# Splitting the q, k and v weights: from VectorE and POOL to ScalarE and VectorE

## The chip, the cores and the metric

The kernel runs on one core of a Trainium2 chip. The metric is the device time of one execution in microseconds (us). The core has a matrix engine (TensorE, PE in the profile), three engines for element-wise work (VectorE = DVE, ScalarE = ACT, GpSimd = POOL) and SyncE (SP), which issues most of the transfers. Each engine works through its own queue of instructions in order; semaphores hold an instruction back until what it needs is there.

## What is computed

Two layers of a transformer over 256 context and 256 latent tokens, width 1024. Each layer has a mixer with three branches (gated delta rule, RG-LRU, differential attention) and a SwiGLU. All branches begin with one projection of the normalised input, `u @ w_in`. What this case is about is the part of it that the delta-rule branch consumes first:

```python
SPLIT = (DN_W, DN_W, DN_H * DN_DV, ...)          # q, k, v: 512 columns each
pc = split_cols(u_c @ w_in)
pl = split_cols(u_l @ w_in)
...
qkv = jax.nn.silu(centred_dwconv(jnp.concatenate([q, k, v], axis=-1), conv_w))
q, k, v = jnp.split(qkv, [DN_W, 2 * DN_W], axis=-1)
q = l2norm(q.reshape(B, T, DN_H, DN_DK))
k = l2norm(k.reshape(B, T, DN_H, DN_DK))
...
g = -jnp.exp(a_log) * jax.nn.softplus(a + dt_bias)   # later: cumsum within chunks
```

## The kernel before

Activations lie with their 1024 features on partitions (8 tiles of 128) and the 512 tokens along the row (context first). Weights come as slabs of 128 output columns: one slab is 128 x 1024 fp32, 0.5 MB, read by SP into a tile `wr` (line 261, three buffers). To keep fp32 accuracy with faster matmuls, both operands are split into a high part in a rounded format and a low part, the rest: `hi` is `wr` rounded (tile `wh`, three buffers, line 264), `lo = wr - hi` (tile `wl`, two buffers, line 265). The product is three matmuls for each of the 8 row blocks: high by high (line 276), high by the activation's low part (line 277), low by high (line 278), so 24 matmuls of 512 columns a slab (256 for q in layer 1, where only latent tokens go on). The activation's parts are `uh` and `ul` (lines 384 to 392).

Which engine rounds and which subtracts is set by the dictionary `how`, whose lists are cycled slab by slab. `how` is updated at the beginning of each stage; the program's order is rearranged by a scheduler at build time, in which the split of a slab has a raised priority (an offset of 400 at line 262) and its load 300.

The stage concerned is `proj` as called by `qkv` and for W_AB and the first LX slab: k, q, v, then the first slab of the RG-LRU. In layer 0 the slabs of W_AB and k are done within the start-up (lines 456 to 465, tiles `whi`, `wlo`, four quarters), in layer 1 those of W_AB and the first k slab at the end of the layer before (`by_halves`); these don't use this entry of `how`. So 9 slabs in layer 0 and 12 in layer 1 go by it.

After each slab's matmuls `conv` empties PSUM twice on ScalarE (`xp`, line 567, and `ta`, line 569; POOL only sets the borders, lines 565 and 566), adds three taps on VectorE (line 573), ScalarE takes a tanh (line 597, `tb`) and VectorE multiplies (line 598, into `kn`, `qn` or `sv`). Psum banks alternate between `mm` and `pg`. Beside this run the units of the modulation weights (`mod_unit`: 1 MB loads `wm` at line 299, matmuls at line 309, a copy `mev` on ScalarE at line 315, transposes at line 318, small VectorE work on `modT` at lines 320 to 328), the softplus of the decay (lines 538 to 546 and 623 to 631), its two cumulative scans (lines 636 and 637, tile `tc`), whose result PE transposes at line 648, and the norms of k and q: squares at line 510, their sums on PE at line 514, scaling at line 604. `sv` is transposed to tokens at line 682.

Of the kernel before, what the change touches and what calls it, by code (L numbers as in the profile page):

```python
# [178 lines left out]
def build(tc, I, out, dbg=None):  # L179
    nc = tc.nc  # L180
    V, S, G, PE, SP = nc.vector, nc.scalar, nc.gpsimd, nc.tensor, nc.sync
# [71 lines left out]
    how = {"hi": [S], "lo": [V]}  # L253
# [220 lines left out]
    for l in range(L):  # L474
# [98 lines left out]
                V.scalar_tensor_tensor(yv, in0=xp[:, :, j:j + 256], scalar=w[:, j:j + 1], in1=yv, op0=ALU.mult, op1=ALU.add)  # L573


        how.update(hi=[V], lo=[G])
        rot[:] = ["mm", "pg"]
        ab = proj(W_AB, ALL)
        spa = tt("tc", WT)
# [657 lines left out]
```

## Time and profile before

| | |
|---|---|
| time, median of 3 runs | 1825.97 us (1821.45 to 1826.0) |
| the profiled execution | 1825.1 us, span 1823.2 us |
| mean granted TensorE clock | 0.983 |
| PE busy, share of the span | 1704.4 us, 93% |
| VectorE busy | 1086.1 us, 60% |
| ScalarE busy | 812.3 us, 45% |
| POOL busy | 263.6 us, 14% |
| `wl` on POOL (line 265) | 32 times, 84.1 us |
| `wh` on VectorE (line 264) | 84 times, 63.1 us |

The busy times are of the whole program, with stages of very different limits; the stage of the change lies at 25 to 165 us and at 1112 to 1225 us. An instruction counts as busy from its start to its end, whatever it does in between.

### The profile page before, as it was taken

Reading aid. Unit: us, or ns where it says so; the run is one execution under the profiler, and the core shown is the slowest. Engines: PE = TensorE matmul, PEld = TensorE weight load, DVE = VectorE, ACT = ScalarE, POOL = GpSimd, SP = SyncE. Lnnn points to the kernel's source line nnn. Section 1 sums busy time; section 2 is a strip of 40 time slices with the busy share of each in tenths; the row PEclk is TensorE's granted clock in tenths of the full one; section 3 lists DMA queues with packets and bytes.
Section 4 is the critical chain, followed back from the end, with each engine's and each line's share of the span. In section 5 each row is a group of like instructions: output and inputs, shape, how many; then the busy total and the mean of one; then the engine's idle time right before and its main releaser. Section 6 shows DMA issues by size and latency. Waiting matters only on the chain.

```text
span 1823.2 us, 27735 instructions
## 1 busy us (share of the span) xinstructions
PE 1704.4 (93%) x10978; PEld 1394.7 (76%) x10978; DVE 1086.1 (60%) x1746; ACT 812.3 (45%) x1416; POOL 263.6 (14%) x291
## 2 busy tenths in 40 slices
PE   6888999999999999999999998788999999999997
PEld 3556787655788887788888886567878679979997
DVE  4677888585453345533333348778885786765554
ACT  4445755553442233332222233347664644444442
POOL 2322000000120013211110004322201002211100
PEclk9999999999999999999999999889999999999999
DMA  9673111435232343323223345432113226555553
GB/s 334 197 250 120 56 47 36 153 116 185 89 97 93 102 146 125 124 93 104 93 94 100 104 136 168 154 105 72 47 46 107 83 88 223 186 180 181 184 185 128
DMA packets 116066, 233.79 MB, mean 128 GB/s; under 512 B 7216, under 2 KB 73148, under 8 KB 115296
## 3 DMA queue, kind: packets, MB, share of 16 engines
q1 hardware_dynamic: 106736, 227.14, 38.4%
q10 hardware_dynamic: 9200, 4.88, 1.0%
q8 instruction: 86, 1.41, 0.3%
q14 instruction: 44, 0.36, 0.1%
HBM read 229.42 MB, written 2.58 MB: 127 GB/s over the span
## 4 chain that ended last, share of the span: by engine, by line
PE 67%; issue 12%; DVE 11%; ACT 5%; DMA 3%; POOL 2%; SPq 0%; POOLq 0%; DVEq 0%; ACTq 0%
PE mm L277 10%; PE mm L276 10%; PE mm L278 10%; PE dn L278 6%; PE dn L276 6%; PE dn L277 6%; PE dn L777 5%; DMA wm<-in_wmod 2%; PE pp L974 1%; PE pg L278 1%; DVE wl L265 1%; DVE ta L573 1%; PE pg L276 1%; PE pg L277 1%; PE md L309 1%
## 5 line engine op out<-in xcount | busy, mean ns | idle before, releaser
L265 DVE TENSOR_TENSOR wl<-wr,wh 128x1024 fp32r<-128x1024 f32 (+1 forms) x270 | 330.1, 1223 | 414.3 <-PE dn L278 171.5
L264 ACT CAST wh<-wr 128x1024 fp32r<-128x1024 f32 (+1 forms) x218 | 225.4, 1035 | 430.1 <-PE mm L277 133.0
L276 PE MATMUL mm<-uh,wh 128*128 128x512 f32 (+1 forms) x1056 | 378.5, 359 | 8.8 <-ACT wh L264 2.6
L277 PE MATMUL mm<-ul,wh 128*128 128x512 f32 (+1 forms) x1056 | 376.8, 357 | 1.9 <-DVE ul L386 1.4
L278 PE MATMUL mm<-uh,wl 128*128 128x512 f32 (+1 forms) x1056 | 374.3, 354 | 4.4 <-DVE wl L265 3.7
L276 PEld LDWEIGHTS mm<-uh,wh 128*128 128x128 f32 x1056 | 203.1, 192 | 37.4 <-issue 6.4
L277 PEld LDWEIGHTS mm<-ul,wh 128*128 128x128 f32 x1056 | 203.0, 192 | 32.7 <-issue 9.4
L278 PEld LDWEIGHTS mm<-uh,wl 128*128 128x128 f32 x1056 | 202.7, 192 | 27.9 <-DVE wl L265 4.3
L277 PE MATMUL dn<-ul,wh 128*128 128x512 f32 (+1 forms) x448 | 151.9, 339 | 0.0
L278 PE MATMUL dn<-uh,wl 128*128 128x512 f32 (+1 forms) x448 | 151.7, 339 | 0.0
L276 PE MATMUL dn<-uh,wh 128*128 128x512 f32 (+1 forms) x448 | 151.6, 338 | 0.0
L265 POOL TENSOR_TENSOR wl<-wr,wh 128x1024 fp32r<-128x1024 f32 x32 | 84.1, 2629 | 139.6 <-PE mm L278 70.2
L277 PEld LDWEIGHTS dn<-ul,wh 128*128 128x128 f32 x448 | 85.2, 190 | 9.5 <-issue 0.4
L276 PEld LDWEIGHTS dn<-uh,wh 128*128 128x128 f32 x448 | 85.1, 190 | 9.4 <-issue 0.4
L278 PEld LDWEIGHTS dn<-uh,wl 128*128 128x128 f32 x448 | 85.3, 190 | 9.2 <-DVE wl L265 0.2
L264 DVE CAST wh<-wr 128x1024 fp32r<-128x1024 f32 x84 | 63.1, 751 | 47.5 <-PE mm L277 30.3
L282 POOL TENSOR_TENSOR hid<-ft,hid 128x512 fp32r<-128x512 f32 (+1 forms) x44 | 44.8, 1018 | 318.8 <-ACT hid L281 318.8
L278 PE MATMUL dn<-hid,wl 128*128 128x256 f32 (+1 forms) x198 | 62.9, 318 | 1.7 <-DVE wl L265 1.7
L276 PE MATMUL mm<-hid,wh 128*128 128x256 f32 (+1 forms) x198 | 62.9, 318 | 0.0
L276 PE MATMUL dn<-hid,wh 128*128 128x256 f32 (+1 forms) x198 | 62.9, 318 | 0.0
L278 PE MATMUL mm<-hid,wl 128*128 128x256 f32 (+1 forms) x198 | 62.9, 318 | 0.0
L278 PE MATMUL pg<-uh,wl 128*128 128x512 f32 (+1 forms) x168 | 62.6, 373 | 0.2 <-POOL wl L265 0.2
(362 smaller groups left out, 3480.2 us busy)
## 6 DMA issues: line engine op xcount, KB each, us to landing
wr<-in_w SPq DMA_DIRECT2D x284, 512.0 KB, 3.8
wm<-in_wmod SPq DMA_DIRECT2D x44, 1024.0 KB, 7.6
wr<-in_w SPq DMA_DIRECT2D x18, 384.0 KB, 3.6
r<-rd SPq DMA_DIRECT2D x5, 1024.0 KB, 5.3
ta<-gd ACTq DMA_DIRECT2D x16, 256.0 KB, 3.6
wm<-in_wmod SPq DMA_DIRECT2D x16, 256.0 KB, 5.3
w<-in_w SPq DMA_DIRECT2D x4, 640.0 KB, 10.3
h<-in_hin SPq DMA_DIRECT2D x8, 256.0 KB, 3.0
```

Of the source, the lines that this page charges most:

```text
L264: (eh.copy if eh is S else eh.tensor_copy)(hi[:, k], r32[:, k])
L265: el.tensor_tensor(lo[:, k], in0=r32[:, k], in1=hi.bitcast(F32)[:, k], op=ALU.subtract)
L276: PE.matmul(ps, lhsT=hi[:, k], rhs=xh[:, tk], start=first and i == 0, stop=False)
L277: PE.matmul(ps, lhsT=hi[:, k], rhs=xl[:, tk], start=False, stop=False)
L278: PE.matmul(ps, lhsT=lo[:, k], rhs=xh[:, tk], start=False, stop=last and i == n - 1)
L282: (eng or G).tensor_tensor(lo, in0=y, in1=hi.bitcast(F32), op=ALU.subtract)
L309: mm = PE.matmul(ps[j:j + 32], lhsT=s_act[:, k], rhs=ts[k // n][:, k % n], start=k < 4, stop=k >= 4, tile_position=(0, j))
L573: V.scalar_tensor_tensor(yv, in0=xp[:, :, j:j + 256], scalar=w[:, j:j + 1], in1=yv, op0=ALU.mult, op1=ALU.add)
L777: PE.matmul(p[:, j], lhsT=lhs[:, j], rhs=rhs[:, j], start=True, stop=True)
L974: PE.matmul(p[:, n], lhsT=gw[:, n, j], rhs=lx[:, j], start=True, stop=True)
```

## The change

One line sets other engines for this stage; the same 21 slabs are split, into the same tiles.

```diff
-        how.update(hi=[V], lo=[G])
+        how.update(hi=[S], lo=[V])
         rot[:] = ["mm", "pg"]
         ab = proj(W_AB, ALL)
```

`V` is VectorE, `G` POOL, `S` ScalarE. The rounding (line 264) becomes a copy on ScalarE, the subtraction (line 265) a VectorE instruction. Since the scheduler orders every queue anew, the split's instructions don't simply change place. Three places show it. The numbers behind a tile's name tell one use of a buffer from another.

VectorE in layer 0's start-up, in the second of the four quarters, where `wh_795` and `wl_796` belong to the first q slab:

```order
-L384 SCALAR_TENSOR_TENSOR nt_279<-h_96,am_82,nrs_171 128x256
-L264 CAST wh_795<-wr_794 128x1024
-L384 SCALAR_TENSOR_TENSOR nt_279<-h_96,am_82,nrs_171 128x256
-L386 SCALAR_TENSOR_TENSOR ul_105<-nt_279,modT_80,uh_104 128x256
-L390 TENSOR_SCALAR nt_286<-nt_286,am_82,modT_80 128x256
-L386 SCALAR_TENSOR_TENSOR ul_105<-nt_279,modT_80,uh_104 128x256
-L390 TENSOR_SCALAR nt_286<-nt_286,am_82,modT_80 128x256
+L384 SCALAR_TENSOR_TENSOR nt_279<-h_96,am_82,nrs_171 128x256 x2
+L390 TENSOR_SCALAR nt_286<-nt_286,am_82,modT_80 128x256 x2
+L265 TENSOR_TENSOR wl_796<-wr_794,wh_795 128x1024
+L386 SCALAR_TENSOR_TENSOR ul_105<-nt_279,modT_80,uh_104 128x256 x2
```

The cast is gone from between the two products `nt`; the subtraction stands behind both `nt` of the odd block and ahead of both `ul`.

VectorE in layer 1 from line 540 on, the run-up to the scans (`wh_10011`, `wl_10012`: the last q slab; 9968 and 9969 the q slab before it; 10056 and 10057 the first v slab):

```order
 L540 TENSOR_SCALAR tb_9825<-ta_9824 128x520
-L264 CAST wh_10011<-wr_10010 128x1024
+L265 TENSOR_TENSOR wl_9969<-wr_9967,wh_9968 128x1024
 L598 SCALAR_TENSOR_TENSOR kn_9565<-tb_9775,ta_9774 128x512
-L320 TENSOR_REDUCE modT_81<-md_9814 128x4
 L321 TENSOR_TENSOR modT_81<-modT_81,vec 128x4
 L325 SCALAR_TENSOR_TENSOR am_85<-modT_81,vec 128x4
+L265 TENSOR_TENSOR wl_10012<-wr_10010,wh_10011 128x1024
 L543 SCALAR_TENSOR_TENSOR tb_9825<-tb_9825,ta_9824 128x520
-L264 CAST wh_10056<-wr_10055 128x1024
 L544 TENSOR_TENSOR tb_9825<-tb_9825,tc_9823 128x520
 L545 SCALAR_TENSOR_TENSOR tb_9826<-tc_9563,tb_9826 128x520
```

Each cast of a slab is replaced by the subtraction of the slab one or two earlier; further down, up to the scans, two more casts (`wh_10117`, `wh_10166`) go and two more subtractions (`wl_10057`, `wl_10118`) come.

ScalarE at the same place in layer 1:

```order
-L315 COPY mev_9812<-md_9803 128x256
+L264 CAST wh_10011<-wr_10010 128x1024
 L541 ACT_TABLE_LOAD
 L541 ACTIVATE tb_9826<-tb_9825 128x520
-L510 ACTIVATE sq_9893<-kn_9565 128x2048
+L264 CAST wh_10056<-wr_10055 128x1024
 L542 ACT_TABLE_LOAD
 L542 ACTIVATE tc_9823<-tb_9826 128x520
+L510 ACTIVATE sq_9893<-kn_9565 128x2048
+L264 CAST wh_10117<-wr_10116 128x1024
 L567 COPY xp_9913<-pg_9852 128x256
```

Three casts come in between the tanh of the last k slab and the first copy of q; the squares of `kn` move behind the second table load, and the copy `mev_9812` has moved ahead of the tanh of line 597. A fourth cast, `wh_10166`, stands ahead of the copy of line 631, which the first scan needs.

## Rows read from the trace of the kernel before

**Rows 1.** Busy time by stretch: length; PE, PEld, DVE, ACT, POOL (instructions); clock; DMA; GB/s

```profile
25.00:60.00 35.00, 31.32 (x182) 20.02 (x182) 18.63 (x48) 11.53 (x32) 15.14 (x14) 0.95 0.73 247
60.00:165.00 105.00, 92.64 (x569) 61.35 (x568) 74.63 (x131) 50.95 (x84) 24.84 (x44) 0.98 0.68 222
1112.00:1165.00 53.00, 45.03 (x304) 33.41 (x305) 37.55 (x54) 17.77 (x33) 23.76 (x26) 0.97 0.58 188
1165.00:1185.00 20.00, 12.58 (x74) 9.24 (x73) 16.81 (x22) 8.97 (x14) 9.17 (x10) 0.80 0.34 107
1185.00:1225.00 40.00, 31.43 (x138) 25.16 (x138) 33.29 (x45) 19.21 (x32) 11.37 (x18) 0.88 0.32 106
```

**Rows 2.** Instructions of lines 265 and 264: count, then ns least/median/most, first and last start

```profile
L265 DVE TENSOR_TENSOR wl<-wr,wh x270: 951/1224/1921, 150.2 to 1807.2; 128x1024 fp32r<-128x1024 f32 x126, 128x768 fp32r<-128x768 f32 x9
...
L265 POOL TENSOR_TENSOR wl<-wr,wh x32: 2371/2666/2911, 32.9 to 1388.3; 128x1024 fp32r<-128x1024 f32 x32
...
L264 ACT CAST wh<-wr x218: 816/1053/1073, 451.4 to 1804.3; 128x1024 fp32r<-128x1024 f32 x100, 128x768 fp32r<-128x768 f32 x9
L264 DVE CAST wh<-wr x84: 666/687/2901, 32.1 to 1514.7; 128x1024 fp32r<-128x1024 f32 x84
```

**Rows 3.** Timeline of POOL in layer 1: start, us, engine, line, operation [idle before <-releaser]

```profile
1165.97 2.40 POOL L265 TENSOR_TENSOR wl<-wr,wh 128x1024 fp32r<-128x1024 f32 x1
```

**Rows 4.** Timeline of VectorE, same columns, around that and elsewhere

```profile
33.10 2.61 DVE L386 SCALAR_TENSOR_TENSOR ul<-nt,modT,uh 128x256 fp32r<-128x256 f32 x1
...
35.96 0.47 DVE L386 SCALAR_TENSOR_TENSOR ul<-nt,modT,uh 128x256 fp32r<-128x256 f32 x1
...
1166.02 2.90 DVE L264 CAST wh<-wr 128x1024 fp32r<-128x1024 f32 x1
...
1176.25 3.35 DVE L636 TENSOR_TENSOR_SCAN tc<-tb,tc 4x512 f32<-4x512 f32 x1
1179.63 1.22 DVE L637 TENSOR_TENSOR_SCAN tc<-tb,tc 4x512 f32<-4x512 f32 x1
...
1218.93 2.83 DVE L573 SCALAR_TENSOR_TENSOR ta<-xp,vec,ta 128x512 f32<-128x512 f32 x1
```

**Rows 5.** PE's waits, 1090 to 1245 us: us in total, times, longest

```profile
PE dn L648 <- DVE tc L637: 7.1, 1, 7.1
PE dn L682 <- DVE sv L598: 4.7, 1, 4.7
PE dn L514 <- ACT sq L510: 3.9, 1, 3.9
PE md L318 <- ACT mev L315: 3.2, 2, 1.7
PE md L309 <- DMA wm<-in_wmod: 2.0, 1, 2.0
```

**Rows 6.** PE's waits, 25 to 185 us

```profile
PE dn L514 <- ACT sq L510: 4.2, 1, 4.2
PE mm L277 <- DVE ul L386: 3.4, 2, 1.7
...
PE md L309 <- ACT ta L569: 1.6, 1, 1.6
```

**Rows 7.** The chain that ended last, in order of time: start us, us, what

```profile
1184.14 0.43 PE pg L276
...
1187.44 0.23 PE pg L278
```

**Rows 8.** VectorE's waits, 25 to 165 us

```profile
DVE wh L264 <- PE mm L277: 4.7, 2, 2.8
...
DVE wh L264 <- PE pg L277: 3.2, 3, 1.7
```

**Rows 9.** VectorE's waits, 1112 to 1240 us

```profile
DVE wh L264 <- PE pg L277: 5.3, 3, 3.0
...
DVE wh L264 <- PE mm L277: 4.1, 3, 2.5
```

## The prediction

> **What bounds the kernel now.** The change touches two stretches, about 25 to 165 us (layer 0) and 1112 to 1225 us (layer 1); so the first view is the busy time of each engine by stretch [rows 1]. PE is busy there for 31.32 of 35, 92.64 of 105, 45.03 of 53, 12.58 of 20 and 31.43 of 40 us: nearly full in layer 0, far from it between 1165 and 1225, where VectorE is busy for 16.81 of 20 and 33.29 of 40 us and the granted clock is down to 0.80 and 0.88. In layer 1's projections VectorE sets the pace.
>
> Much of this VectorE time is no work. POOL's low-part subtraction takes 2.67 us (median of 32), the same operation on VectorE 1.22 us [rows 2]. Now lay POOL's and VectorE's instructions of the same microseconds side by side [rows 3, 4]: POOL subtracts from 1165.97 to 1168.37, and VectorE's cast of line 264, begun at 1166.02, takes 2.90 us instead of 0.69. The scan of line 636 takes 3.35 us, its twin of line 637 behind it 1.22. `ul` takes 2.61 us at 33.10 and 0.47 us at 35.96. While POOL subtracts, a VectorE instruction that begins is held until POOL ends. The list of waits doesn't show this, because the held instruction counts as busy. I went through VectorE's instructions beside all 21 POOL subtractions that the change removes and took from each stretched one the duration of its like that ran alone: 22 instructions, the first at 33.10, the last at 1218.93, hold 41.6 us too much (15.9 in layer 0, 25.7 in layer 1).
>
> Third, what this does to PE: the list of PE's waits. Layer 1 [rows 5]: 7.1 us for the scan (line 637 before the transposes of line 648), 4.7 for `sv`, 3.9 for the squares that hang on `kn`, 3.2 for `mev`, 2.0 for a load of `wm`. Layer 0 [rows 6]: 4.2 for the squares, 3.4 for `ul`, 1.6 for `ta`. Behind long waits matmuls of 512 columns step at 0.43 us instead of 0.23 [rows 7]: that is the lower of the two levels, 1.2 against 2.4 GHz.
>
> **The change, part by part.** 21 slabs are concerned: layer 0 has W_AB and the k slabs from the start-up, so 9 (q, v, the first LX); layer 1 has W_AB and the first k slab from its entry, so 12.
>
> POOL loses 21 x 2.67 = 56 us. VectorE loses 21 casts of 0.69 and gains 21 subtractions of 1.22 [rows 2], +11.1 us, and loses the 41.6 us of being held: 30.5 us less. ScalarE gains 21 casts of 1.05 [rows 2], 22.1 us; it is busy for 50.95 of 105 us and for 8.97 of 20 and 19.21 of 40 us [rows 1], so there is room but no free passage, since its queue is in order.
>
> What of this lies on PE's path, by stretch:
>
> 25 to 60: the order shows `wl` ahead of `ul` on VectorE in two of the three quarters. Before, `ul` came behind a cast and its own holding, 0.69 + 2.14 us; after, behind a 1.22 us subtraction, so 1.6 us earlier, twice: 3.2 of the 3.4 us of waits.
>
> 60 to 165: the wait for `ta` (1.6) hangs on a `kn` product that is held for 2.2 us; taken whole. The wait for the squares (4.2) has three held instructions ahead of it (6.5 us), against which three subtractions cost 3 x 0.53 more: 4.9 earlier at most; I take 3, since ScalarE has two more casts there. Sum 4.6.
>
> 1112 to 1165: the `wm` load (2.0) was issued late because SP's queue is in order and stood on buffers that POOL freed late; `mev` (3.2) stood behind a tanh that waited for held convolutions, and in the new order it is ahead of that tanh. I take 4 of 5.2.
>
> 1165 to 1185: between line 540 and the scans four instructions are held, 8.7 us together. Four subtractions in the place of four casts cost 2.1 more there, and two of the new ScalarE casts (`wh_10056` ahead of the second table load, `wh_10166` ahead of the copy that the scan needs) another 2.1: 8.7 - 2.1 - 2.1 = 4.5 of the 7.1 us.
>
> 1185 to 1225: four held instructions (8.0 us) against 4 x 0.53: 5.9 of the 8.6 us.
>
> Sum of waits 3.2 + 4.6 + 4 + 4.5 + 5.9 = 22.2 us. **The clock**: by the granted means [rows 1] the low level cost at most 0.05 x 35 + 0.02 x 105 + 0.03 x 53 + 0.20 x 20 + 0.12 x 40 = 14.2 us, part of it while PE stood still; it fell behind the waits that shrink. Between 0 and 14.2 I take 5, since waits of 2 to 3 us stay.
>
> **What it gives back**: a new cast waits in ScalarE's queue until PE has let go of the slab three back, and at several places stands just ahead of the copy out of PSUM (lines 567 and 569) of the slab that PE has just finished. The same wait stood in VectorE's queue: 4.7, 3.2, 5.3 and 4.1 us [rows 8, 9]. In its place VectorE's new subtraction waits for PE's end of the slab two back, which is about the same moment; I cost this move at nothing, and if that cover is missing it costs those 17.3 us. The casts themselves: of 19 not yet counted one in five on the path, 19 x 1.05 / 5 = 4 us; the bounds are 0 and 20 us.
>
> The sum: 22.2 + 5 - 4 = 23 us less. The profiled execution took 1825.1 us, 0.9 under the median of the three; 1826.0 - 23 = **1803 us**.
>
> A rule speaks against the change: the Trainium skill (Perfetto Trace Analysis, Optimizing Scalar/DVE Operations) has it that what VectorE does in one of its faster modes should stay there unless VectorE is saturated. The trace agrees on the price (0.69 against 1.05 us) [rows 2]; VectorE at 84% with a third of it held [rows 1] is not saturated by work, so by the rule the cast should have stayed and only the subtraction moved, and the change would lose 21 x 0.37 = 7.8 us that I count only where a cast is on the path.
>
> **Rivals.** (a) PE's clock recovers wholly: 22.2 + 14.2 = 36 us, 1790 us. For it: the low level stands only behind the named waits. Against: 2 to 3 us of wait are left at the scan and the squares. (b) ScalarE takes over as the engine waited for: its casts on the path give back 14 to 27 us of the 27.2, 1813 to 1826 us. For it: it evacuates every slab, and its queue is in order. Against: under 49% busy in these stretches [rows 1]. (c) Slower: the casts and the waits in front of them come onto the path whole, 22.1 + 17.3 = 39.4 us against 22.2 + 5 gained: 12 us more, 1838 us. The place is layer 1 from the k slabs to the scans, where tanh, softplus and evacuation share ScalarE; it decides from the point at which more than 27 of these 39 us are on PE's path. Against it: a wait by PE for VectorE or ScalarE is 7.1 us at the longest now, and the cast is away from VectorE at every such place. (d) The loads set the pace: PE comes earlier to the `wm` units than their 1 MB loads (one wait for DMA of 2.0 us [rows 5], and a DMA share of 0.68 in layer 0 [rows 1]); then layer 0's 4.6 and the 4 of 1112 to 1165 go, and with them the clock: 23 - 13.6 = 9 us, 1817 us. That the change wouldn't do what it says is out: the order has no subtraction of these slabs on POOL any more.
>
> **How the numbers follow.** Forecast (1793 to 1812) 0.60; (a) 0.15; (b) 0.15, a third of it within 0.3%; (c) 0.05; (d) 0.05. 0.3% (5.5 us) is about what a measurement of this kernel can tell from no change. Faster by more: 0.60 + 0.15 + 0.10 + 0.05 = 0.90; within: 0.05; slower: 0.05. The range reaches to (a) and into (b) and (d): 1788 to 1817 us.
>
> **What would show it.** In the profile after: POOL's group of line 265 has 11 instructions left; VectorE has no scan of 3.35 us and no 2.6 us `ul`; its busy time falls by some 30 us and ScalarE's rises by 22; PE's wait for line 637 falls from 7.1 to about 3 us and the granted clock between 1165 and 1225 rises over 0.9. The prediction is wrong if PE's waits name ScalarE's `xp` or `ta` instead, if the held VectorE instructions turn out to have had slack behind them, or if the other POOL instructions hold VectorE as much as the removed ones.

## The result and the profile after

The changed kernel takes 1792.47 us (median of 4 runs, 1790.19 to 1794.81) against 1825.99 us before in the same comparison: ratio 0.983, 95% interval 0.981 to 0.985, 33.5 us less. The forecast was 1803, the range 1788 to 1817. A second comparison gave 1796.4 us for the same kernel, ratio 0.984 (0.982 to 0.986): between two comparisons the changed kernel moves by 4 us, so 30 to 34 us are gained.

First the engines over the whole program, from the page of the changed kernel (busy time, share of the span of 1788.4 us, instructions):

```profile
PE 1692.2 (95%) x10978; PEld 1390.1 (78%) x10978; DVE 1063.0 (59%) x1746; ACT 830.6 (46%) x1437; POOL 207.2 (12%) x270
```

PE runs the same 10978 matmuls in 1692.2 us instead of 1704.4, and stands still for 1788.4 - 1692.2 = 96.2 us instead of 1823.2 - 1704.4 = 118.8. So of the 34.8 us of the profiled executions 12.2 are PE's busy time and 22.6 are waits. The 12.2 us are the clock: the mean granted clock is 0.990 after and 0.983 before, and PE's busy time times the granted clock is about 1675 us in both. VectorE's busy time fell by 23.1 us, ScalarE's rose by 18.3, POOL's fell by 56.4.

Busy time by stretch, the answer to [rows 1] (the same columns; each stretch is cut where PE has run as many matmuls as at the borders there, to within a few, so it lies earlier):

```profile
25.50:54.50 29.00, 28.72 (x183) 19.27 (x182) 19.36 (x49) 13.79 (x37) 11.09 (x12) 1.00 0.85 290
54.50:151.50 97.00, 90.79 (x568) 61.21 (x568) 67.92 (x131) 55.98 (x90) 5.91 (x38) 1.00 0.73 241
1095.30:1140.50 45.20, 43.40 (x306) 33.69 (x306) 30.15 (x55) 23.11 (x38) 7.95 (x21) 0.96 0.69 222
1140.50:1153.90 13.40, 10.87 (x74) 8.76 (x72) 11.40 (x17) 9.83 (x15) 0.34 (x4) 1.00 0.48 157
1153.90:1191.20 37.30, 29.44 (x142) 23.43 (x139) 29.43 (x47) 23.21 (x38) 4.07 (x17) 0.92 0.34 113
```

PE stands still for 0.3, 6.2, 1.8, 2.5 and 7.9 us of these stretches; before it was 3.7, 12.4, 8.0, 7.4 and 8.6. The granted clock is 1.00 in three of the five. Only the last stretch waits about as long as before, at a clock of 0.92 against 0.88.

Lines 265 and 264, the answer to [rows 2]:

```profile
L265 DVE TENSOR_TENSOR wl<-wr,wh x291: 951/1225/3394, 33.3 to 1772.8; 128x1024 fp32r<-128x1024 f32 x137, 128x768 fp32r<-128x768 f32 x9
...
L265 POOL TENSOR_TENSOR wl<-wr,wh x11: 2367/2432/2759, 679.1 to 1354.4; 128x1024 fp32r<-128x1024 f32 x11
```

```profile
L264 ACT CAST wh<-wr x239: 817/1053/1067, 31.4 to 1770.0; 128x1024 fp32r<-128x1024 f32 x111, 128x768 fp32r<-128x768 f32 x9
L264 DVE CAST wh<-wr x63: 662/686/696, 132.6 to 1480.5; 128x1024 fp32r<-128x1024 f32 x63
```

21 subtractions left POOL, which keeps 11, and 21 casts went to ScalarE. Before, the longest VectorE cast took 2901 ns; now the longest takes 696.

VectorE's timeline at the places of [rows 4] (start us, us, engine, line, operation):

```profile
34.43 1.85 DVE L386 SCALAR_TENSOR_TENSOR ul<-nt,modT,uh 128x256 fp32r<-128x256 f32 x2
...
1150.10 1.20 DVE L636 TENSOR_TENSOR_SCAN tc<-tb,tc 4x512 f32<-4x512 f32 x1
1151.34 1.22 DVE L637 TENSOR_TENSOR_SCAN tc<-tb,tc 4x512 f32<-4x512 f32 x1
```

The first scan takes 1.20 us instead of 3.35. Two `ul` together take 1.85 us; alone they take 0.87, so here 1.0 us of holding is left, beside POOL's own `ul` of line 392, which the change leaves alone.

PE's waits in layer 1, 1070 to 1225 us, the answer to [rows 5] (total, times, longest):

```profile
PE dn L682 <- DVE sv L598: 6.5, 2, 4.6
...
PE dn L514 <- ACT sq L510: 1.4, 1, 1.4
PE dn L648 <- DVE tc L637: 1.4, 1, 1.4
PE pg L276 <- ACT ta L569: 1.2, 1, 1.2
```

and in layer 0, 25 to 180 us, the answer to [rows 6]:

```profile
PE dn L682 <- DVE sv L598: 2.3, 1, 2.3
...
PE md L318 <- ACT mev L315: 1.7, 2, 1.0
PE mm L276 <- ACT uh L385: 1.3, 1, 1.3
PE mm L277 <- DVE ul L386: 1.1, 1, 1.1
```

The wait for the scan has fallen from 7.1 to 1.4 us, those for the squares from 4.2 and 3.9 to 0 and 1.4, the one for the `wm` load from 2.0 to 0.3; the one for `sv` in layer 1 has grown, from 4.7 to 6.5. In both stretches together all of PE's waits add up to 40.9 us before and 19.7 after.

### The profile page after: what moved, and what is told of

The parts are those of the page before. It is cut to its first block, busy times and chain, and to the rows that moved or that the text cites. A ratio compares the mean times of both kernels' runs of the same rounds, so it can differ in the third digit from the quotient of the medians.

```text
span 1788.4 us, 27733 instructions
## 1 busy us (share of the span) xinstructions
PE 1692.2 (95%) x10978; PEld 1390.1 (78%) x10978; DVE 1063.0 (59%) x1746; ACT 830.6 (46%) x1437; POOL 207.2 (12%) x270
## 4 chain that ended last, share of the span: by engine, by line
PE 69%; issue 11%; DVE 10%; ACT 5%; DMA 3%; POOL 1%; SPq 0%; POOLq 0%; ACTq 0%; DVEq 0%
PE mm L277 10%; PE mm L276 10%; PE mm L278 10%; PE dn L278 7%; PE dn L276 7%; PE dn L277 7%; PE dn L777 5%; DMA wm<-in_wmod 2%; DVE wl L265 1%; PE pg L277 1%; PE pg L278 1%; PE pg L276 1%; PE pp L974 1%; PE md L309 1%; PE dn L309 1%
## 5 line engine op out<-in xcount | busy, mean ns | idle before, releaser
L265 DVE TENSOR_TENSOR wl<-wr,wh 128x1024 fp32r<-128x1024 f32 (+1 forms) x291 | 358.7, 1233 | 430.6 <-PE dn L278 176.2
L264 ACT CAST wh<-wr 128x1024 fp32r<-128x1024 f32 (+1 forms) x239 | 247.5, 1036 | 438.2 <-PE mm L277 139.9
L276 PE MATMUL pg<-uh,wh 128*128 128x512 f32 (+1 forms) x168 | 62.0, 369 | 1.2 <-ACT ta L569 1.2
L276 PE MATMUL mm<-hid,wh 128*128 128x256 f32 (+1 forms) x198 | 62.9, 318 | 0.0
L276 PE MATMUL dn<-hid,wh 128*128 128x256 f32 (+1 forms) x198 | 62.9, 318 | 0.0
L277 PE MATMUL mm<-hid,wh 128*128 128x256 f32 (+1 forms) x198 | 62.6, 316 | 0.0
L277 PE MATMUL dn<-hid,wh 128*128 128x256 f32 (+1 forms) x198 | 62.5, 316 | 0.0
```

Source lines behind the costliest of these rows:

```text
L264: (eh.copy if eh is S else eh.tensor_copy)(hi[:, k], r32[:, k])
L265: el.tensor_tensor(lo[:, k], in0=r32[:, k], in1=hi.bitcast(F32)[:, k], op=ALU.subtract)
L276: PE.matmul(ps, lhsT=hi[:, k], rhs=xh[:, tk], start=first and i == 0, stop=False)
L277: PE.matmul(ps, lhsT=hi[:, k], rhs=xl[:, tk], start=False, stop=False)
```

## The experiments

The theory, H: a POOL instruction that reads tiles makes a VectorE instruction that begins meanwhile stand until it ends, and most of the gain is the end of that. Two rivals: L, the low part and the buffers `wr` and `wl` were late because POOL was slow, and PE and the loads waited for that; W, VectorE simply had too much to do.

All times stand beside runs of the kernel before on the same chip, which took 1826.0 to 1826.9 us. "PE idle" is the span minus PE's busy time. The busy and idle times are those of the one profiled execution, which can lie some us off the median: after's is the fastest of its four (1790.2 us) and e9's of its four (1794.8), e8's is the slowest of its four (1845.8).

| kernel | us, median | ratio, 95% | PE busy | PE idle | VectorE busy |
|---|---|---|---|---|---|
| before | 1826.0 | 1 | 1704.4 | 118.8 | 1086.1 |
| after | 1792.5 | 0.981 to 0.985 | 1692.2 | 96.2 | 1063.0 |
| e12, after again | 1796.4 | 0.982 to 0.986 | 1695.8 | 100.1 | 1063.2 |
| e1, cast alone | 1818.9 | 0.994 to 0.998 | 1707.9 | 112.2 | 1069.8 |
| e2, subtraction alone | 1799.1 | 0.984 to 0.987 | 1697.8 | 103.5 | 1066.5 |
| e5, idle subtraction | 1807.8 | 0.987 to 0.991 | 1698.0 | 108.3 | 1089.3 |
| e6, idle memsets | 1796.7 | 0.982 to 0.985 | 1695.6 | 100.3 | 1063.1 |
| e8, two idle subtractions | 1841.1 | 1.006 to 1.009 | 1718.5 | 125.5 | 1121.1 |
| e9, start-up back | 1799.9 | 0.983 to 0.988 | 1694.6 | 98.4 | 1061.2 |
| e4, layer 1 alone | 1807.7 | 0.988 to 0.992 | 1701.3 | 108.2 | 1067.6 |
| e7, POOL splits no slab here | 1790.6 | 0.979 to 0.982 | 1694.7 | 94.1 | 1060.3 |
| e10, `ul` too | 1792.1 | 0.980 to 0.984 | 1694.5 | 95.7 | 1058.3 |
| e11, all low parts | 1789.0 | 0.978 to 0.982 | 1696.0 | 92.0 | 1097.7 |

**Each half alone.** The rounding alone (e1), the subtraction alone (e2):

```diff
-        how.update(hi=[V], lo=[G])
+        how.update(hi=[S], lo=[G])   # e1
+        how.update(hi=[V], lo=[V])   # e2
```

> Half of the change: the cast goes to ScalarE, the subtraction stays on POOL. VectorE loses 21 x 0.69 = 14 us of work, nothing else. Theory H: the held time stays, so little comes of it, 1815 to 1826 us. Rival W (VectorE's load is what counts, whatever takes it off): 14 of 30 us of relief, so about half of the gain, 1806 to 1812 us.

> The other half: the cast stays on VectorE, the subtraction goes from POOL to VectorE. VectorE gets 21 x 1.22 = 26 us of work more and loses the 42 us of being held. Theory H: 16 us of VectorE's time net, about half to most of the gain, 1796 to 1808 us. Rival W (what helps is work that leaves VectorE for an engine with room): VectorE has more to do than before, 1826 us or above.

e1 gained 7 us, e2 27. In e2 VectorE has all of the work, 21 casts and 21 subtractions, so W, by which it had too much to do, falls: taking work off VectorE (e1) is worth a quarter of giving it more without POOL (e2). PE's waits in layer 1 of e1, 1090 to 1245 us:

```profile
PE pg L276 <- ACT ta L569: 5.2, 1, 5.2
PE dn L682 <- DVE sv L598: 5.2, 2, 4.0
PE dn L514 <- ACT sq L510: 3.9, 1, 3.9
```

The squares are as late as in [rows 5], 3.9 us: POOL still subtracts. What the cast adds to e2 is 3 to 7 us by the medians. Up to the end of layer 0's projections and from line 581 to 728 in layer 1 the traces of e2 and after differ by only 1.1 us (148.05 against 148.85 us, and 88.2 against 86.3); the other 11.8 us of the two spans arise outside these stretches, where the two profiles of the changed kernel also differ by 7.5 us, and the intervals of e2 and after overlap. So the cast's share is small and not settled. By the Trainium skill (Perfetto Trace Analysis, Optimizing Scalar/DVE Operations) a VectorE performance mode is faster where there is one, and moving work to ScalarE may make sense if VectorE is saturated; with VectorE busy for 59% that speaks for e2. The run shows nothing of the 7.8 us by which e2 would then be faster: it is 3 to 7 us slower by the medians.

**An idle reader on POOL.** e5 is the changed kernel with one useless subtraction on POOL for each slab of this stage. It waits only for the slab's cast, touches a tile of its own, nobody waits for it, and the queues of PE, VectorE, ScalarE and SP hold the same instructions in the same order as after. e6 has three memsets in its place, which take POOL longer but only write; e8 has two subtractions, again with the other queues in e5's order:

```diff
+            ci = (the cast of line 264)
+            if extra[0] is not None:
+                z = extra[0]                     # a tile that is not in use yet
+                after(G.tensor_tensor(z, in0=z, in1=z, op=ALU.subtract), ci)   # e5; e8: twice
+                for _ in range(3): after(G.memset(z, 0.0), ci)                 # e6, in its place
```

The first three of these, in layer 0, come only after the start-up, since the tile is free only then.

> The kernel after, and for each of the 21 slabs one more POOL subtraction of 128x1024 whose result nobody uses: it reads and writes a tile of its own and waits only for the slab's cast, so it keeps no weight buffer. The queues of PE, VectorE and ScalarE are in the same order as in the kernel after; only POOL has more to do (in layer 0 the first three come after the start-up). Theory H (a POOL subtraction holds VectorE while it runs): VectorE instructions are held for about 2 us each again, some 35 us together, and the time goes from 1792 to between 1808 and 1820 us. Rival L (the gain came because POOL delivered the low part, and freed the weight buffer, later than VectorE does): POOL's result is not waited for, the time stays within 3 us of 1792.

> As the run with the idle subtraction, but in its place POOL fills the same tile three times (128x1024 memset, about 1 us each by the 0.53 us of a 128x512 one): as long a time on POOL, at the same places, that only writes. If only a POOL instruction that reads holds VectorE, the time stays within 4 us of 1792. If any busy POOL holds VectorE, or if its small border fills coming late are what costs, it is as slow as the run with the idle subtraction, 1808 to 1820 us.

> The changed kernel with two idle POOL subtractions for each slab, some 4 us in place of the 2 us of one; the queues of the other engines keep the order they have with one. If the gain is that VectorE is no longer held, the cost grows with the time that POOL reads: one gave back 15.3 us, two give back 25 to 31 us, 1818 to 1823 us, and VectorE's busy time is 45 to 55 us over the changed kernel's. If the cost of the idle subtractions lies in POOL's own queue (borders and parts that come late), it is at most twice that of the three memsets (4.3 us for 3 us of POOL a slab), so under 1801 us.

e5's timeline of POOL and of VectorE in the run-up to the scans (its line 268 is the idle subtraction; 550 and 634 are lines 546 and 628 of the listing):

```profile
1154.95 4.89 POOL L268 TENSOR_TENSOR oacc<-oacc 128x1024 f32<-128x1024 f32 x2 [2.28 <-ACT wh L265]
```

```profile
1155.70 2.39 DVE L550 TENSOR_TENSOR tc<-tb,tb 128x520 f32<-128x520 f32 x1
1158.12 1.75 DVE L634 TENSOR_SCALAR sm<-tc 128x8 f32<-128x8 f32 x1
```

In the changed kernel these two take 0.69 and 0.17 us. Here they stand while POOL reads a tile that has nothing to do with them, even the one of 8 columns. In e6 POOL's memsets lie beside the scans themselves (POOL, then VectorE):

```profile
1152.06 5.17 POOL L269 MEMSET oacc<- 128x1024 f32 x5 [1.04 <-ACT wh L265]
```

```profile
1152.33 0.71 DVE L635 TENSOR_SCALAR sm<-tc 128x8 f32<-128x8 f32 x1
...
1155.54 1.20 DVE L643 TENSOR_TENSOR_SCAN tc<-tb,tc 4x512 f32<-4x512 f32 x1
1156.78 1.22 DVE L644 TENSOR_TENSOR_SCAN tc<-tb,tc 4x512 f32<-4x512 f32 x1
```

The scans take 1.20 and 1.22 us, and VectorE is busy for 1063.1 us, as after. The time of e6, 1796.7, is 0.7 us over the bound it was given, but that of the changed kernel within its spread (1796.4 in e12). Only the small `sm` and the `tc` behind it are stretched, by 1.0 us together. This agrees with the Trainium skill (SBUF — State Buffer, Who interferes with whom): a VectorE instruction with two SBUF inputs contends with a POOL instruction that reads SBUF, not with one that only writes, while one in a two-port mode can contend with either, and whoever comes second stands until the other has ended. Whether it is such a mode that makes `sm` stand beside the memsets, no run here shows.

So H is shown. In e5 18 instructions are held for 26 us, not for the some 35 us that were expected, and its 1807.8 us lie at the lower edge of what H was given (1808 to 1820). The place is the right one too: with the idle subtraction PE's wait at line 648 is back, with two the one at line 514 as well. PE's waits in e5, 1090 to 1245 us, and in e8, 1090 to 1290 us (654 and 518 are lines 648 and 514):

```profile
PE dn L654 <- DVE tc L643: 5.9, 1, 5.9
PE dn L518 <- ACT sq L514: 2.2, 1, 2.2
```

```profile
PE dn L518 <- ACT sq L514: 5.2, 1, 5.2
PE dn L654 <- DVE tc L643: 5.0, 1, 5.0
```

e8 came out 18 us above the upper end of what H was expected to give, and VectorE's busy time 3 us above its range: I had doubled the cost of e5, and it rose to three or four times that. VectorE's busy time over the changed kernel's is 26 us in e5 and 58 in e8, the time over the changed kernel's 11 to 15 and 45 to 49 us. In the profiled executions PE's idle time grows somewhat faster than the holding, by 8 to 12 and 25 to 29 us; the steep part is PE's busy time for the same matmuls, 2 to 6 against 23 to 26 us more: the longer waits also bring the clock down, to a mean of 0.987 in e5 and 0.973 in e8 from 0.990 and 0.988 in the two runs of the changed kernel. The other three runs of e8 had 0.978 to 0.979; for its median the clock's part is then 15 to 20 us (an estimate, from the 1675 us above).

The kernel before has 41.6 us of holding, between the two. On the straight line between e5 and e8 that is 28 to 31 us, of the 30 to 34 that were gained; this is an estimate, and since the price rises faster than the holding, rather too high a one. What is left for L, late buffers and low parts, which the idle subtractions don't imitate, is small: in the trace of before PE waits for POOL's low part itself for 0.8 us in layer 1 (1112 to 1229 us) and not at all in layer 0:

```profile
PE mm L278 <- POOL wl L265: 0.6, 1, 0.6
...
PE pg L278 <- POOL wl L265: 0.2, 1, 0.2
```

But the waits for `mev` (3.2 us) and for the `wm` load (2.0) in layer 1 come back neither in e5 nor in e8. These 5 us are not the holding's; they belong to the new order of the queues or to buffers that come free earlier, and no run parts the two.

**The start-up.** e9 is the changed kernel with the first three slabs of layer 0 split as before:

```diff
-        how.update(hi=[S], lo=[V])
+        how.update(hi=[V] * 3 + [S] * 6 if full else [S], lo=[G] * 3 + [V] * 6 if full else [V])
```

> The changed kernel in which the first three slabs of layer 0 (the q slabs split within the start-up, 30 to 60 us) are split as before: VectorE rounds, POOL subtracts. The other 18 slabs are as changed. If the start-up's 6.3 us of the gain are those three slabs' and stay to the end, 1798.8 us. If only the 3.2 us of the prediction hang on them and the rest is something else (other order of the queues, the clock), 1795.5 us. If layer 0 absorbs an earlier start behind its loads, 1793 us.

The end of the start-up (VectorE's line 581) moves from 58.16 to 63.28 us; before it was at 64.43. POOL and VectorE there, and PE's wait (25 to 185 us):

```profile
31.76 2.56 POOL L265 TENSOR_TENSOR wl<-wr,wh 128x1024 fp32r<-128x1024 f32 x1 [3.96 <-DVE wh L264]
```

```profile
31.99 2.60 DVE L386 SCALAR_TENSOR_TENSOR ul<-nt,modT,uh 128x256 fp32r<-128x256 f32 x1
```

```profile
PE mm L277 <- DVE ul L386: 3.3, 2, 1.7
```

The held `ul` and the wait of [rows 6] are back, and with them 5.1 of the start-up's 6.3 us. They stay through layer 0's projections: line 728 is reached at 154.8 us, against 148.85 after. At the end of the program 3 to 7 us are seen, by which of the two medians of the changed kernel one takes; the runs of e9 spread from 1794.8 to 1804.7. That the start-up's gain belongs to these slabs is shown, its size at the end only roughly.

**Layer 1 alone.** e4 has the new setting in layer 1 and the old one in layer 0:

```diff
+        how.update(hi=[V] if full else [S], lo=[G] if full else [V])
```

> The change in layer 1 alone (12 slabs); layer 0 keeps the VectorE cast and the POOL subtraction. If the two layers' gains are separate and what the traces show (start of the span to the last projection of layer 0: 14.7 us; from there on 18.8 us), 1826 - 18.8 = 1807 us. By the prediction's own terms for layer 1 (4 + 4.5 + 5.9 of waits, 3.4 of the 5 for the clock, 2 given back by ScalarE) 1826 - 15.8 = 1810 us. If instead layer 1 is quicker only because layer 0 hands over its loads and its clock in a better state, 1815 us or more.

1807.7 us, 18.8 us under before: as the traces had it, the layers' gains add up, to within the some 3 us of the interval; layer 0 alone was not run. The 1810 us by the prediction's own terms lie in that interval too; that layer 1 gains only through layer 0 is out.

**Further off POOL.** e7 takes the eight low parts behind layer 1's projections off POOL too, e10 also the `ul` of line 392, e11 also the low parts of line 282; e12 is the changed kernel beside e10 and e11.

```diff
-        how.update(hi=[V], lo=[V] if full else [V, G])
+        how.update(hi=[V], lo=[V])                                       # e7, e10, e11
-                        G.tensor_tensor(lo[:, sl], in0=t[:, sl], ...)
+                        V.tensor_tensor(lo[:, sl], in0=t[:, sl], ...)    # e10, e11
-        (eng or G).tensor_tensor(lo, in0=y, ...)
+        (eng or V).tensor_tensor(lo, in0=y, ...)                         # e11
```

> The changed kernel, in which the stage behind the projections in layer 1 also takes its eight low parts from POOL to VectorE; POOL keeps three in the whole program. If what counts is that a POOL subtraction holds VectorE: about 8 us of held instructions disappear between 1181 and 1357 us, PE waits there for only 11 us in all, so 2 to 4 us less than 1792.5: 1789 us. If what counts is how much VectorE has to do: it gains 8 x 1.22 = 9.8 us at a busy share of 78% there, and the time rises to 1793 to 1797 us.

> As e7 (the eight low parts behind layer 1's projections on VectorE too), and the low parts of the activation of line 392 move from POOL to VectorE: 28 POOL instructions of 1.0 us become 28 VectorE ones of some 0.47 us (the duration of line 386). If holding is what costs: the three holds of 1.0 us that are left in the start-up and PE's wait of 1.1 us for ul go, 1 to 3 us under e7: 1787.5 to 1789.5 us. If VectorE's own work is now the limit there: 12 x 0.47 us more in the start-up's chain, 1791 to 1796 us.

> As e10, and line 282's low parts (SwiGLU, the mix, the attention's output) leave POOL for VectorE as well, 92 us of POOL in the whole program; POOL keeps the products of line 389, masks, copies and memsets. If holding costs wherever it happens, a few us less than e10. But PE is busy for 391 of 400 us between 600 and 1000 us, where most of them lie, so there is little to win: within 2 us of e10 is expected. If VectorE's added work (some 40 us) comes onto the path in the mix and attention's output, 2 to 6 us more.

> The changed kernel itself, beside the two variants on the same chip: 1792.5 us again, between 1790 and 1795, as a base for differences of 1 to 3 us.

e12, the same kernel again, lies 1.4 us above what was expected of it, so differences of 1 to 3 us can't be read off single medians. On the same chip e10 is 4.3 and e11 7.4 us under the changed kernel (1796.4); e11's interval, 0.978 to 0.982, just doesn't meet that of e12, 0.982 to 0.986. e7 and e10 can't be told from after or from each other; where the start-up's `ul` went to VectorE, PE waits longer for `uh` instead (2.4 us against 1.2), so taking the 1.0 us holds away there bought nothing. e11 is the best that was run, 1789.0 us. Its engines:

```profile
PE 1696.0 (95%) x10978; PEld 1392.8 (78%) x10978; DVE 1097.7 (61%) x1860; ACT 830.8 (46%) x1437; POOL 70.4 (4%) x156
```

VectorE has 35 us more to do than in after, POOL 137 less, and PE is idle for 92.0 us, the least of all. That line 282 has little to give (within 2 us of e10) is neither borne out nor refuted: e11 is 3 us under e10, with intervals that overlap.

## Why the prediction was right, and where its sizes were off

The mechanism was right, and so was its place. By the same instruction in both traces (line 581 in each layer, the scan of line 637, the first line 728), in us:

| piece | before | after | gained | forecast, without clock and ScalarE |
|---|---|---|---|---|
| start-up, to line 581 | 64.43 | 58.16 | 6.3 | 3.2 |
| layer 0, to line 728 | 163.54 | 148.85 | 8.4 | 4.6 |
| up to line 581 of layer 1 | 1124.92 | 1108.23 | 2.0 | 0 |
| layer 1, to the scan of line 637 | 1179.63 | 1151.34 | 11.6 | 4 + 4.5 |
| to line 728 | 1228.17 | 1194.52 | 5.4 | 5.9 |
| to the end | 1823.2 | 1788.4 | 1.1 | 0 |

- **The waits.** 22.2 us of them were to go and ScalarE to give 4 back, so 18.2 net; 40.9 - 19.7 = 21.2 us went. Two terms were mis-sized, and they partly cancel. In 1185 to 1225 5.9 of the 8.6 us for `sv` and the squares were to go, but 7.9 are left (6.5 and 1.4). And of the 4 us that ScalarE was to give back nothing is seen on balance. The other four terms came to 18.7 us (`ul` 2.3, layer 0's `ta` and squares 5.8, `wm` and `mev` 4.9, the scan 5.7) against 16.3. New casts are on the path, but few. In the chain of waits that ended last, in layer 1 (start us, us, what):

```profile
1141.28 0.94 ACT wh L264
...
1145.52 1.14 DVE wl L265
...
1158.47 0.96 ACT wh L264
```

  The first is the cast ahead of the second table load, which was foreseen. Yet PE's wait for line 637 fell to 1.4 us, not to 3. Other instructions ahead of it, among them a tap and three small ones on `modT` between 1127 and 1157 us, were held by some 2 us each as well, and I counted only the four behind line 540; that this is the reason is likely, not shown.
- **The clock.** 5 us were taken between bounds of 0 and 14.2. By the working of the prediction the five stretches of after still lose 0.04 x 45.2 + 0.08 x 37.3 = 4.8 us, so 14.2 - 4.8 = 9.4 came back; PE's busy time in them fell from 213.0 to 203.2 us, by 9.8. In the second profile of the changed kernel only the last of the five is under 1.00 (0.93), and 11.6 us came back. So the term was about half of what it should have been, the largest part of the miss: start-up and layer 0 are at 1.00 although waits of 1 to 2 us stay, which I had held against it. The forecast that the clock between 1165 and 1225 would rise over 0.9 holds: over the same work it went from 0.86 to 0.94. But in the last stretch, where `sv` is still late, 0.92 is left. From the scan of line 637 to line 728, 5.4 us were gained, and 4.7 of them are PE's busy time (38.6 to 34.0 us, for 161 and 157 matmuls), only 0.8 its waits: the 5.9 in the table came near by luck. So rival (a), the nearest by its time (1790 us), was right for three of the five stretches, and its clock did not recover wholly.
- **21.2 + 9.4 = 30.6** of the 31.7 us that the two stretches gained. The 3.1 us outside them I can't assign; the two profiles of the changed kernel differ by 7.5 us themselves.
- **VectorE's busy time** was to fall by 30 us and fell by 23. Of the 41.6 us of holding by these subtractions nothing is left, but new holds came, 7.2 us in all. The new subtractions delay `ul` and other instructions into POOL's work of lines 392 and 389, beside which 8.2 us are held instead of 3.1. And the last of four taps at 1180 us meets one of POOL's remaining subtractions (POOL, then VectorE):

```profile
1181.70 2.66 POOL L265 TENSOR_TENSOR wl<-wr,wh 128x1024 fp32r<-128x1024 f32 x1 [7.60 <-PE pg L278]
```

```profile
1180.09 4.82 DVE L573 SCALAR_TENSOR_TENSOR ta<-xp,vec,ta 128x512 f32<-128x512 f32 x4
```

  That tap takes 2.83 us instead of 0.74, and in the chain that ended last it stands right before the `sv` that PE waits 4.6 us for:

```profile
1182.08 2.83 DVE ta L573
...
1185.43 0.69 DVE sv L598
...
1186.17 1.13 PE dn L682 x4
```

  In e7, where this subtraction has left POOL, the longest wait for `sv` is 2.9 us. I had counted the holds that go, not those that come. ScalarE's busy time rose by 18.3 us, not by 22.
- **Rivals (b), (c), (d).** PE's waits name ScalarE with 1.2 to 1.7 us each, so it did not become the bound. The change did not come out slower. The loads did not set the pace: layer 0 gave more than forecast, not less.

## What to carry over

Read VectorE's durations beside POOL's before believing a busy share: an instruction that takes several times what its like takes alone, and ends when POOL's ends, is standing. Then a slow engine's help has two prices, its own duration and the time for which it holds the fast engine, and on a path that PE waits for the second is paid too. Count the holds that a change brings as well as those that it takes away. Where the clock fell behind waits, price its return by stretch, over the same work before and after: here it came back to 1.00 in layer 0, where PE's longest wait is 2.3 us, and only to 0.92 behind the scans, where one of 4.6 us is left.

## What was not expected

The holding depends on whether POOL reads, far more than on how long it is busy: 62 us of memsets hold VectorE for 1.0 us and cost nothing that can be measured, 51 us of subtractions cost 11 to 15 us. It falls on VectorE instructions of any size (0.17 us became 1.75). And its price rises faster than its length, 26 us of holding for 11 to 15 us and 58 for 45 to 49, since the granted clock goes down with it: in the profiled executions PE's busy time for the same matmuls rises by 2 to 6 us in the one case and by 23 to 26 in the other.
